# A map's scores of the differential heads in one three-bank PSUM tile, with a softmax over whole rows

## The chip, the cores and the metric

The kernel runs on one core of a Trainium2 chip. Its engines work from queues of their own: TensorE (PE: matrix products, with weight loads shown as PEld), VectorE (DVE), ScalarE (ACT), GpSimd (POOL) and SyncE (SP), which here issues nearly all DMAs. Matrix products land in PSUM, which this kernel uses as eight banks of 512 fp32 columns on 128 partitions. The metric is the device time of one execution in microseconds (us), the median of three runs.

## What is computed

One step of a backbone of two layers over 128 context tokens and 1024 latent tokens, 1024 channels. The first layer is a state-space and pooling mixer, the second one mixes differential attention (8 heads) with windowed attention (16 heads). The change lies in the differential heads. Cut to what matters (the running of `block` over blocks of 128 queries, the projections and the norms are left out):

```python
def diff_attention(q, k, v, lam):
    scale = DIFF_HD ** -0.5

    def block(qb):
        s = jnp.einsum('bhiqd,bhikd->bhiqk', qb, k).astype(jnp.float32) * scale
        p = jax.nn.softmax(s, axis=-1)
        attn = p[:, :, 0] - lam * p[:, :, 1]
        return jnp.einsum('bhqk,bhkv->bhqv', attn.astype(v.dtype), v)
```

A head has two maps (i = 0, 1), each with its own query and key of 64 channels. A latent query reads 128 cached context keys and 1024 latent keys, 1152 in all; the 128 context queries read the 128 context keys.

## The kernel before

Tokens run along the columns of channel-major tiles, in nine blocks of 128 (`NCH`): block 0 is the context, blocks 1 to 8 the latents. Products of fp32 accuracy are made of fp16 pairs (a high and a low part): a projection is three matmuls for each of eight 128-channel slices (`mm3`, lines 330 to 332).

The second layer (`odd`) runs the eight differential heads, then eight blocks of windowed heads, then the output projection. While head h runs its attention, the projections of head h+1 (K, Q and V) and one gate (Z) are worked off by `Filler`: `F.take` hands out projection matmuls to fill TensorE's time between pieces of attention. TensorE's order is the program's; the other engines' orders come from a scheduler, with instructions under `high_priority` put first. `qk_block` projects K or Q and rotates it (`evac`): ScalarE copies the product to `raw`, VectorE multiplies by cosines, VectorE shuffles, GpSimd multiplies by sines and adds, then ScalarE and GpSimd split the result, held in the one buffer `q32`, into its high and low part; SP copies these into the layout that the score matmuls want.

`diff_head` goes over the nine query blocks. For each of the two maps it makes the scores in three chunks of 384 columns (`CH3`; one of 128 for block 0), each chunk in its own PSUM bank (`S1`, which rotates over five banks by `SCORE_BANKS`). VectorE takes a maximum for each chunk (line 1282) and combines the three (1286); ScalarE takes three exponentials with their sums into SBUF (1289). After each map `F.take` gives TensorE a sixteenth of the projections. Then VectorE adds the sums, and combines the two maps in three products (1303); ScalarE and GpSimd split the result into high and low (1306, 1307), and a transposing DMA turns it for the product with the values (1227). That product, `diff_pv`, is put into the queue `pend`, and worked off after the first map of a later block, when more than two entries wait: the block that is three back is done then. It writes into a bank of its own (`sm`), from which ScalarE copies it (1325).

PSUM in this stage: `mm` two banks for projections, `S1` three, `s4` one, `m3` one and `sm` one. The score rotation is these lines:

```python
SCORE_BANKS = ("S1", "s4", "S1", "m3", "S1")
self.banks = {"mm": ["mm"], "S1": list(SCORE_BANKS)}
```

The windowed heads use `mm`, `m3`, `S1`, `s4` and `sm` as well, and take over without a break: the last three value products of head 7 are worked off inside the first windowed block. `odd_setup` loads the cached values (`cv`, lines 1136 to 1141) before the first rotation, through a `q32` buffer.

Of the kernel before, what the change touches and what calls it, by code (L numbers as in the profile page):

```python
# [10 lines left out]
F32 = mybir.dt.float32  # L11
# [37 lines left out]
SCORE_BANKS = ("S1", "s4", "S1", "m3", "S1")  # L49
# [172 lines left out]
class Builder:  # L222
# [291 lines left out]
    def prologue(self):  # L514
# [3 lines left out]
        self.evps.enter_context(self.psum("evps", ss=4, ada=1))  # L518
# [608 lines left out]
    def odd_setup(self):  # L1127
# [8 lines left out]
        self.cv = self.wt([P, 2, 10, P], F16, tag="cv", bufs=1)  # L1136
        t = self.tl(self.rot, [P, TK], F32, "q32", 1)
        nc.sync.dma_start(t, A["cv"])
        cvf = self.cv.rearrange("p a b c -> p a (b c)")
        nc.scalar.activation(cvf[:, 0], t, AF.Copy)  # L1140
        nc.vector.tensor_tensor(cvf[:, 1], t, cvf[:, 0], ALU.subtract)

# [10 lines left out]
        nc.vector.tensor_scalar(self.nsink, self.row("sink"), -1.0, None, ALU.mult)  # L1153

    def qk_block(self, key, src, hs, cache=None, kout=None, scale=1.0, pre=None):
# [7 lines left out]
        def evac(ps, c0, c1):  # L1163
# [7 lines left out]
            nc.vector.scalar_tensor_tensor(q[:, c0 + o:c1], ps[:, o:], scale, self.cosT[:, a:b], ALU.mult, ALU.mult)  # L1171
# [84 lines left out]
    def diff_head(self, h, F):  # L1256
# [8 lines left out]
        for b in range(NCH):  # L1265
            nk = 1 if b == 0 else 9
            w = nk * P
            qs = slice(b * P, (b + 1) * P)
            p = []
            sm = self.wt([P, 16], F32, tag="sms", bufs=6)  # L1270
            part = ((0, P),) if b == 0 else CH3
            for m in range(2):
                ss = []
                mx = self.wt([P, 4], F32, tag="mx", bufs=4)
                nb = sm[:, m:m + 1]
                for j, (c0, c1) in enumerate(part):
                    sv = self.pt("S1")[:, :c1 - c0]
                    o = TC if b else 0
                    for x in range(2):
                        nc.tensor.matmul(sv, q[:, m, x, qs], k[:, m, o + c0:o + c1], start=x == 0, stop=x == 1)  # L1280
                    with self.tc.high_priority():
                        nc.vector.tensor_reduce(out=mx[:, j:j + 1], in_=sv, axis=AX.X, op=ALU.max)  # L1282
                    ss.append(sv)
                pm = self.wt([P, T], F32, tag="p", bufs=4)
                with self.tc.high_priority():
                    nc.vector.tensor_reduce(out=nb, in_=mx[:, 0:len(part)], axis=AX.X, op=ALU.max, negate=True)  # L1286
                    for j, (c0, c1) in enumerate(part):
                        i = 8 + m * 3 + j
                        nc.scalar.activation(pm[:, c0:c1], ss[j], AF.Exp, bias=nb, accum_out=sm[:, i:i + 1])  # L1289
                p.append(pm)  # L1290
                F.take(HEAD_FIRST if b == 0 else left / 16)
                if m == 0:
                    self.pop(2)

            phl = self.wt([P, 2 * T], F16, tag="phl", bufs=2)
            with self.tc.high_priority():
                n = len(part)
                nc.vector.tensor_reduce(out=sm[:, 4:6], in_=sm[:, 8:14].rearrange("p (a b) -> p a b", a=2)[:, :, 0:n],
                                        axis=AX.X, op=ALU.add)
# [7 lines left out]
            nc.gpsimd.tensor_tensor(phl[:, w:2 * w], p[0][:, :w], phl[:, :w], ALU.subtract)  # L1307
# [334 lines left out]
```

## Time and profile before

| | us |
|---|---|
| median of three runs (2294.38 to 2300.79) | 2299.93 |
| the profiled execution | 2299.1 |
| its span, from first to last instruction | 2297.3 |
| TensorE busy (88% of the span) | 2031.8 |
| VectorE busy (67%) | 1534.2 |
| ScalarE busy (56%) | 1293.6 |
| GpSimd busy (46%) | 1067.8 |
| differential heads, first to last score matmul | 679.8 |

The mean granted clock of TensorE is 0.954 of full speed. Busy shares are means over stages with different limits, so what a stage costs is read from its own stretch: how long each engine is busy in it, and in which waits TensorE, which does most of the work, stands still.

### The profile page before, as it was taken

The numbers are of one execution on the slowest core, as the hardware profiler recorded it, in microseconds if no ns is written. First come the engines' busy times: TensorE is split into PE (matmuls) and PEld (weight loads), VectorE is DVE, ScalarE is ACT, GpSimd is POOL, SyncE is SP. The second block draws the span as 40 slices with busy tenths as digits, with TensorE's granted clock in tenths as the row PEclk, the third lists the DMA queues.
The fourth block names the chain that finished last, engine by engine and source line by source line (L and its number), as shares of the span: only waits on it lengthen the run. The fifth ranks groups of instructions, "written<-read, shape, count | busy, mean of one in ns | idle before, by whom it ended". The sixth has DMA issues, their size and how long they took to land. (4 is left out here: it accounts for less than half of the span.)

```text
span 2297.3 us, 50851 instructions
## 1 busy us (share of the span) xinstructions
PE 2031.8 (88%) x20258; PEld 1452.5 (63%) x20258; DVE 1534.2 (67%) x3329; ACT 1293.6 (56%) x3530; POOL 1067.8 (46%) x997
## 2 busy tenths in 40 slices
PE   4997788787999999978898998988977999898997
PEld 2654475564557555656686676775766777686566
DVE  5868989789585444747877777778785545552334
ACT  5575666666363311436666666666676777773321
POOL 1378677876674100134445445345345656552001
PEclk9998899998999999999999999999999999999999
DMA  7221514224657522135555455544556786899412
GB/s 275 70 80 50 147 58 111 82 80 131 222 184 209 174 71 86 40 102 114 97 125 115 96 113 116 105 107 105 105 124 133 151 168 143 171 180 205 155 47 83
DMA packets 434990, 283.17 MB, mean 123 GB/s; under 512 B 374432, under 2 KB 385216, under 8 KB 434752
## 3 DMA queue, kind: packets, MB, share of 16 engines
q1 hardware_dynamic: 433776, 279.34, 49.7%
q8 instruction: 158, 2.59, 0.5%
q10 hardware_dynamic: 976, 0.58, 0.1%
q14 instruction: 80, 0.66, 0.1%
HBM read 133.38 MB, written 29.05 MB: 71 GB/s over the span
## 5 line engine op out<-in xcount | busy, mean ns | idle before, releaser
L330 PE MATMUL psmm<-h,whl 128*128 128x384 f16 (+1 forms) x1104 | 369.9, 336 | 16.7 <-DVE q L1171 11.5
L331 PE MATMUL psmm<-h,whl 128*128 128x384 f16 (+1 forms) x1104 | 368.7, 335 | 2.3 <-DVE h L507 1.7
L332 PE MATMUL psmm<-h,whl 128*128 128x384 f16 (+1 forms) x1104 | 368.7, 335 | 0.0
L330 PE MATMUL psmm<-whl,h 128*128 128x128 f16 x1920 | 345.9, 224 | 0.0
L331 PE MATMUL psmm<-whl,h 128*128 128x128 f16 x1920 | 345.7, 224 | 0.0
L332 PE MATMUL psmm<-whl,h 128*128 128x128 f16 x1920 | 345.4, 224 | 0.0
L330 PEld LDWEIGHTS <-whl 128*128 128x128 f16 x2256 | 226.6, 100 | 162.0 <-issue 23.6
L332 PEld LDWEIGHTS <-whl 128*128 128x128 f16 x2256 | 225.4, 100 | 157.1 <-issue 18.6
L331 PEld LDWEIGHTS <-whl 128*128 128x128 f16 x2256 | 225.9, 100 | 151.6 <-issue 27.6
L1307 POOL TENSOR_TENSOR phl<-p,phl 128x1152 f16<-128x1152 f32 (+1 forms) x72 | 159.9, 2221 | 249.8 <-ACT phl L1306 210.2
L330 PEld LDWEIGHTS <-h 128*128 128x128 f16 x2520 | 250.9, 100 | 9.4 <-issue 3.8
L331 PEld LDWEIGHTS <-h 128*128 128x128 f16 x2520 | 250.8, 100 | 6.9 <-issue 1.2
L332 PEld LDWEIGHTS <-h 128*128 128x128 f16 x2520 | 250.8, 100 | 0.0
L324 DVE SCALAR_TENSOR_TENSOR whl<-w,whl 128x512 f16<-128x512 f32 x248 | 191.0, 790 | 67.6 <-ACT whl L323 67.1
L1385 POOL TENSOR_TENSOR phl<-p,phl 128x1024 f16<-128x1024 f32 (+2 forms) x72 | 135.0, 1876 | 117.6 <-ACT phl L1384 117.2
L323 ACT ACTIVATE whl<-w 128x512 f16<-128x512 f32 x248 | 140.6, 609 | 78.8 <-PE psmm L332 42.3
L1289 ACT ACTIVATE p<-psS,sms 128x384 f32<-128x384 f32 (+1 forms) x240 | 136.0, 569 | 66.0 <-DVE sms L1286 65.6
L1174 POOL TENSOR_TENSOR sw<-sw,sin 128x384 f32<-128x384 f32 (+1 forms) x78 | 87.4, 1121 | 154.2 <-DVE sw L1173 126.4
L1303 DVE SCALAR_TENSOR_TENSOR p<-p,sms,p 128x384 f32<-128x384 f32 (+1 forms) x200 | 151.9, 793 | 2.5
L1282 DVE TENSOR_REDUCE mx<-psS 128x1 f32<-128x384 f32 (+1 forms) x240 | 125.2, 540 | 37.4 <-PE psS L1280 37.4
L1280 PEld LDWEIGHTS <-Q 128*128 128x128 f16 x800 | 73.7, 98 | 117.6 <-issue 82.4
L504 POOL TENSOR_TENSOR h<-mt,h 128x384 f16<-128x384 f32 (+2 forms) x32 | 29.1, 919 | 252.8 <-ACT h L503 252.8
(396 smaller groups left out, 6122.8 us busy)
## 6 DMA issues: line engine op xcount, KB each, us to landing
w<-in_wod SPq DMA_DIRECT2D x52, 512.0 KB, 3.7
w<-in_wev SPq DMA_DIRECT2D x40, 512.0 KB, 4.0
E<-csrow SPq DMA_DIRECT2D x36, 512.0 KB, 3.9
Q<-qhl SPq DMA_DIRECT2D x64, 288.0 KB, 4.6
go_dr<-gl SPq DMA_DIRECT2D x15, 576.0 KB, 3.3
wada<-in_w_ada SPq DMA_DIRECT2D x32, 256.0 KB, 5.4
o<-in_w_ada SPq DMA_DIRECT2D x16, 512.0 KB, 5.8
xT<-in_w_ada SPq DMA_DIRECT2D x16, 512.0 KB, 6.5
```

Of the source, the lines that this page charges most:

```text
L323: nc.scalar.activation(hl[:, 0, a:e], w[:, a:e], AF.Copy if scale is None else AF.Identity, scale=sc)
L324: nc.vector.scalar_tensor_tensor(hl[:, 1, a:e], w[:, a:e], sc, hl[:, 0, a:e], ALU.mult, ALU.subtract)
L330: mm(out, ah, bh, start=start, stop=False)
L331: mm(out, ah, bl, start=False, stop=False)
L332: mm(out, al, bh, start=False, stop=stop)
L1174: nc.gpsimd.tensor_tensor(sw[:, o:], sw[:, o:], self.sinT[:, a:b], ALU.mult)
L1280: nc.tensor.matmul(sv, q[:, m, x, qs], k[:, m, o + c0:o + c1], start=x == 0, stop=x == 1)
L1282: nc.vector.tensor_reduce(out=mx[:, j:j + 1], in_=sv, axis=AX.X, op=ALU.max)
L1289: nc.scalar.activation(pm[:, c0:c1], ss[j], AF.Exp, bias=nb, accum_out=sm[:, i:i + 1])
L1303: nc.vector.scalar_tensor_tensor(p[0][:, c0:c1], p[1][:, c0:c1], sm[:, 2:3], p[0][:, c0:c1], ALU.mult, ALU.add)
L1307: nc.gpsimd.tensor_tensor(phl[:, w:2 * w], p[0][:, :w], phl[:, :w], ALU.subtract)
L1385: nc.gpsimd.tensor_tensor(phl[:, 2 * w:4 * w], p, phl[:, :2 * w], ALU.subtract)
```

## The change

In the differential heads a map's scores go into one PSUM tile of three banks (`S`, 1536 columns, two buffers): 1152 columns of scores as two matmuls of 512 columns and one of 128, for each of the two parts of the query. VectorE takes one maximum over the whole row, ScalarE one exponential with its sum; the first map's exponential goes to SBUF, the second one's is written over its own scores in PSUM. One VectorE product then combines the two, and one ScalarE copy makes the high part. The value product of an earlier block goes into columns 1152 to 1279 of the first map's tile, ahead of that map's scores, and ScalarE copies it out after that map's exponential (`diff_out`). With the two projection banks this is all of PSUM, so the windowed heads' tiles are opened only when the score tiles are closed: the first windowed K and Q and all value products that still wait are finished before that. `m3` moves into the first layer's pool and the windowed heads' one. In the stage ahead of head 0 the projections rotate over `S`, `S`, `mm`, `mm` in place of `m3`, `S1`, `mm`, `mm`. The cached values are loaded after head 0's projections, and head 0's K is rotated from the copy `raw` where its product was made ahead (`pre`). The diff, cut to its core:

```diff
 def pt(self, tag, shape=(P, 512)):
-        p, b = (self.ps, 2 if tag == "mm" else 1) if tag in ("mm", "m3") else (self.ps2, self.psb[tag])
+        p, b = (self.ps, 2) if tag == "mm" else (self.ps2, self.psb[tag])
 def qk_block(self, key, src, hs, cache=None, kout=None, scale=1.0, pre=None):
...
-            nc.vector.scalar_tensor_tensor(q[:, c0 + o:c1], ps[:, o:], scale, self.cosT[:, a:b], ALU.mult, ALU.mult)
+            if pre is None:
+                nc.vector.scalar_tensor_tensor(q[:, c0 + o:c1], ps[:, o:], scale, self.cosT[:, a:b], ALU.mult, ALU.mult)
+            else:
+                nc.vector.tensor_tensor(q[:, c0 + o:c1], raw[:, o:], self.cosT[:, a:b], ALU.mult)
 def diff_head(self, h, F):
...
-            part = ((0, P),) if b == 0 else CH3
             for m in range(2):
-                ss = []
-                mx = self.wt([P, 4], F32, tag="mx", bufs=4)
+                st = self.pt("S", [P, 1536])
+                sv = st[:, :w]
+                out = self.pend.popleft()(st) if m == 0 and len(self.pend) > 2 else None
                 nb = sm[:, m:m + 1]
-                for j, (c0, c1) in enumerate(part):
-                    sv = self.pt("S1")[:, :c1 - c0]
-                    o = TC if b else 0
+                for c0 in range(0, w, 512):
+                    c1 = min(c0 + 512, w)
                     for x in range(2):
-                        nc.tensor.matmul(sv, q[:, m, x, qs], k[:, m, o + c0:o + c1], start=x == 0, stop=x == 1)
-                    with self.tc.high_priority():
-                        nc.vector.tensor_reduce(out=mx[:, j:j + 1], in_=sv, axis=AX.X, op=ALU.max)
-                    ss.append(sv)
-                pm = self.wt([P, T], F32, tag="p", bufs=4)
+                        nc.tensor.matmul(sv[:, c0:c1], q[:, m, x, qs], k[:, m, o + c0:o + c1], start=x == 0, stop=x == 1)
+                e = self.wt([P, T], F32, tag="p", bufs=4)[:, :w] if m == 0 else sv
                 with self.tc.high_priority():
-                    nc.vector.tensor_reduce(out=nb, in_=mx[:, 0:len(part)], axis=AX.X, op=ALU.max, negate=True)
-                    for j, (c0, c1) in enumerate(part):
-                        i = 8 + m * 3 + j
-                        nc.scalar.activation(pm[:, c0:c1], ss[j], AF.Exp, bias=nb, accum_out=sm[:, i:i + 1])
-                p.append(pm)
+                    nc.vector.tensor_reduce(out=nb, in_=sv, axis=AX.X, op=ALU.max, negate=True)
+                    nc.scalar.activation(e, sv, AF.Exp, bias=nb, accum_out=sm[:, 4 + m:5 + m])
+                p.append(e)
+                if out is not None:
+                    out()
                 F.take(HEAD_FIRST if b == 0 else left / 16)
-                if m == 0:
-                    self.pop(2)
...
-                for c0, c1 in part:
-                    nc.vector.scalar_tensor_tensor(p[0][:, c0:c1], p[1][:, c0:c1], sm[:, 2:3], p[0][:, c0:c1],
-                                                   ALU.mult, ALU.add)
-                for c0, c1 in part:
-                    nc.scalar.activation(phl[:, c0:c1], p[0][:, c0:c1], AF.Copy)
+                nc.vector.scalar_tensor_tensor(p[0], p[1], sm[:, 2:3], p[0], ALU.mult, ALU.add)
+                nc.scalar.activation(phl[:, :w], p[0], AF.Copy)
...
+    def diff_pv(self, st, h, b, nk, pt, sm, og, oss):
-        po = self.pt("sm")
+        po = (self.pt("S", [P, 1536]) if st is None else st)[:, T:T + P]
...
+        if st is not None:
+            return lambda: self.diff_out(po, h, b, sm, og, oss)
+        self.diff_out(po, h, b, sm, og, oss)
 def odd(self, hs, pre):
...
-                odps.enter_context(self.psum("odps", S1=3, s4=1, sm=1))
-                self.banks = {"mm": ["m3", "S1", "mm", "mm"]}
+                odps.enter_context(self.psum("dfps", S=2))
+                self.banks = {"mm": ["S", "S", "mm", "mm"]}
                 F.add("first", first(), 28.0)
                 F.until("first")
-                self.banks = {"mm": ["mm"], "S1": list(SCORE_BANKS)}
+                self.banks = {"mm": ["mm"]}
+                self.cached_values()
                 for h in range(8):
...
+                F.until(("wk", 0))
+                F.until(("q", 8))
+                self.pop(0)
+                odps.close()
+                odps.enter_context(self.psum("odps", S1=3, m3=1, s4=1, sm=1))
```

`cached_values` is the load and split of `cv` taken out of `odd_setup`, word for word; `diff_out` is the end of the old `diff_pv` from its copy on.

What this moves, first on VectorE, in a block of a middle head around the first V projection. Before (1282 is the maximum of a chunk, 1286 their combination, 1298 the sum of sums, 1300 and 1301 the scalars of the combination, 1303 the combination itself, 1205 the low part of V):

```order
L1282 TENSOR_REDUCE mx_18091<-pss_2206_18092 128x1
L1298 TENSOR_REDUCE sms_17904<-sms_17904 128x2
L1282 TENSOR_REDUCE mx_18091<-psS_2207_18096 128x1
L1282 TENSOR_REDUCE mx_18091<-psm_2208_18100 128x1
L1300 RECIPROCAL sms_17904<-sms_17904 128x2
L1205 SCALAR_TENSOR_TENSOR V_17950<-psmm_17958,V_17950 128x384
L1286 TENSOR_REDUCE sms_18090<-mx_18091 128x1
L1301 SCALAR_TENSOR_TENSOR sms_17904<-sms_17904,lms_11493 128x1
L1303 SCALAR_TENSOR_TENSOR p_17918<-p_18021,sms_17904,p_17918 128x384 x3
L1282 TENSOR_REDUCE mx_18197<-psS_2215_18198 128x1
```

After (1290 is the maximum of a row, 1299 and 1300 the scalars, 1301 the combination, 1210 the low part of V):

```order
L1301 SCALAR_TENSOR_TENSOR p_17102<-psS_17162,sms_17067,p_17102 128x1152
L1290 TENSOR_REDUCE sms_17230<-psS_17231 128x1
L1210 SCALAR_TENSOR_TENSOR V_17135<-psmm_17143,V_17135 128x384
L1290 TENSOR_REDUCE sms_17230<-psS_17328 128x1
L1210 SCALAR_TENSOR_TENSOR V_17135<-psmm_17279,V_17135 128x384
L1299 RECIPROCAL sms_17230<-sms_17230 128x2
L1300 SCALAR_TENSOR_TENSOR sms_17230<-sms_17230,lms_11488 128x1
L1301 SCALAR_TENSOR_TENSOR p_17265<-psS_17328,sms_17230,p_17265 128x1152
L1290 TENSOR_REDUCE sms_17399<-psS_17400 128x1
```

Before, the maxima of the next block's first map stand ahead of the combination; now each combination stands ahead of them.

Second on SP's queue ahead of head 0 (`q<-in_cv` is the load of the cached values, `q<-in_ckT` that of a head's cached keys, K and Q the copies into the score layout, w a weight block). Before:

```order
L1132 DMA sin_11482<-in_sin 128x1024
L1134 DMA mask_11484<-in_mask 128x896
L1138 DMA q_1358_11487<-in_cv 128x1280
L1161 DMA q_1362_11503<-in_ckT 128x128
L1179 DMA out_dk<-q_1362_11503 128x128
L313 DMA w_1465_12286<-in_wod 128x1024
L1187 DMA K_11717<-qhl_11714 64x1280 x4
```

After:

```order
L1133 DMA mask_11484<-in_mask 128x896
L1163 DMA q_1360_11498<-in_ckT 128x128
L1184 DMA out_dk<-q_1360_11498 128x128
L312 DMA w_1446_12234<-in_wod 128x1024
L1192 DMA K_11712<-qhl_11709 64x1280 x4
L312 DMA w_1468_12595<-in_wod 128x1024
L1197 DMA Q_11825<-qhl_11822 64x2x1152
L312 DMA w_1503_13050<-in_wod 128x1024
L1197 DMA Q_11825<-qhl_11822 64x2x1152 x3
L1152 DMA q_1392_11906<-in_cv 128x1280
L1163 DMA q_1393_11910<-in_ckT 128x128
```

The load has moved from ahead of head 0's keys to behind head 0's queries, and ahead of head 1's keys.

## Rows read from the trace of the kernel before

**Rows 1.** Stretches: us, busy PE PEld DVE ACT POOL, PE clock, DMA, GB/s.

```profile
1038.30:1718.10 679.80, 609.19 (x6807) 476.04 (x6808) 532.32 (x1296) 455.79 (x1390) 310.14 (x185) 0.96 0.52 109
1295.00:1340.00 45.00, 35.33 (x308) 24.86 (x306) 37.92 (x90) 28.44 (x82) 27.78 (x18) 0.95 0.45 98
1340.00:1383.00 43.00, 43.00 (x584) 37.18 (x583) 29.96 (x78) 29.58 (x97) 12.13 (x6) 0.98 0.57 120
1718.10:1741.00 22.90, 19.20 (x183) 13.60 (x182) 14.60 (x42) 14.68 (x50) 11.05 (x9) 1.00 0.53 114
```

**Rows 2.** What line 1280 (scores) waited for: us in total, times.

```profile
  ACT p L1289: 69.1, 36
```

**Rows 3.** TensorE's timeline: start, us, line, operation; idle time before it in brackets.

```profile
1302.49 0.22 PE L1322 MATMUL pssm<-V,PT 128*128 128x128 f16 x1
...
1304.00 0.49 PE L1280 MATMUL pss<-K,Q 128*128 128x384 f16 x2
...
1304.97 0.33 PE L330 MATMUL psmm<-h,whl 128*128 128x384 f16 x1
...
1307.90 0.81 PE L1280 MATMUL psS<-K,Q 128*128 128x384 f16 x4
...
1316.20 0.48 PE L1280 MATMUL psS<-K,Q 128*128 128x384 f16 x2 [2.48 <-ACT p L1289]
...
1322.85 0.48 PE L1280 MATMUL psS<-K,Q 128*128 128x384 f16 x2 [2.59 <-ACT p L1289]
...
1336.09 0.80 PE L1280 MATMUL psm<-K,Q 128*128 128x384 f16 x2 [3.82 <-ACT p L1289]
```

**Rows 4.** Timelines of GpSimd, VectorE and ScalarE just before 1316 us.

```profile
1309.17 2.61 POOL L1182 TENSOR_TENSOR qhl<-q,qhl 128x1280 f16<-128x1280 f32 x1
...
1309.28 2.54 DVE L375 TENSOR_SCALAR rqy<-oss 128x9 int32<-128x9 int32 x1
...
1313.78 1.01 DVE L1282 TENSOR_REDUCE mx<-psS 128x1 f32<-128x384 f32 x2
...
1315.48 0.58 ACT L1289 ACTIVATE p<-psS,sms 128x384 f32<-128x384 f32 x1 [3.38 <-DVE sms L1286]
```

**Rows 5.** Durations: two lines of VectorE (ns min/median/max, whole run), two timeline rows.

```profile
L1303 DVE SCALAR_TENSOR_TENSOR p<-p,sms,p x200: 331/614/2969, 1048.0 to 1723.9; 128x384 f32<-128x384 f32 x96, 128x128 f32<-128x128 f32 x4
L1171 DVE SCALAR_TENSOR_TENSOR q<-psmm,cos x68: 408/547/559, 1003.3 to 2016.0; 128x384 f32<-128x384 f32 x42, 128x256 f32<-128x256 f32 x26
1318.81 1.36 DVE L1243 TENSOR_TENSOR og<-og,orr 128x1152 f32<-128x1152 f32 x1
1735.89 0.67 ACT L1375 ACTIVATE p<-psS,sms 128x512 f32<-128x512 f32 x1
```

**Rows 6.** The stretch behind the 3.82 us wait (columns as in rows 1).

```profile
1338.00:1342.00 4.00, 4.00 (x41) 4.00 (x40) 2.68 (x8) 3.03 (x9) 0.73 (x1) 0.51 0.85 166
```

**Rows 7.** Timelines of SP, ScalarE and TensorE ahead of head 0.

```profile
993.95 0.43 SPq L1138 DMA_DIRECT2D q<-in_cv  x1
...
1000.45 1.27 ACT L1140 ACTIVATE cv<-q 128x1280 f16<-128x1280 f32 x1 [6.36 <-DMA q<-in_cv]
...
1003.89 0.50 PE L330 MATMUL psmm<-h,whl 128*128 128x384 f16 x1 [11.46 <-DVE q L1171]
...
1031.39 2.59 SPq L1192 DMA_DIRECT2D Q<-qhl  x3
...
1038.32 0.37 PE L1280 MATMUL psS<-K,Q 128*128 128x128 f16 x2 [3.64 <-DMA Q<-qhl]
```

**Rows 8.** Timelines of GpSimd and TensorE behind the last differential scores.

```profile
1723.74 2.43 POOL L1307 TENSOR_TENSOR phl<-p,phl 128x1152 f16<-128x1152 f32 x1 [8.35 <-ACT phl L1306]
...
1730.83 0.23 PE L1322 MATMUL pss<-V,PT 128*128 128x128 f16 x1 [1.86 <-DMA PT<-phl]
```

**Rows 9.** VectorE's busy time in lines 1303, then 1282, in 1295 to 1340.

```profile
1295.00:1340.00 45.00, 9.90 (x11) 0.95 0.45 98
1295.00:1340.00 45.00, 11.91 (x24) 0.95 0.45 98
```

More of the change, by code (lines that the diff above doesn't have):

```diff
@@ L48 @@
 WIN_FIRST, WIN_SHIFT = 1.5, 1.0
-SCORE_BANKS = ("S1", "s4", "S1", "m3", "S1")
 NE = 5
@@ L517, in prologue @@
         self.evps = ExitStack()
-        self.evps.enter_context(self.psum("evps", ss=4, ada=1))
+        self.evps.enter_context(self.psum("evps", ss=4, ada=1, m3=1))
         with self.scope("pro"):
@@ L1153, in odd_setup, with cached_values @@
         nc.vector.tensor_scalar(self.nsink, self.row("sink"), -1.0, None, ALU.mult)
+    def cached_values(self):
+        nc, A = self.nc, self.A
+        self.cv = self.wt([P, 2, 10, P], F16, tag="cv", bufs=1)
+        t = self.tl(self.rot, [P, TK], F32, "q32", 1)
+        nc.sync.dma_start(t, A["cv"])
+        cvf = self.cv.rearrange("p a b c -> p a (b c)")
+        nc.scalar.activation(cvf[:, 0], t, AF.Copy)
+        nc.vector.tensor_tensor(cvf[:, 1], t, cvf[:, 0], ALU.subtract)
     def qk_block(self, key, src, hs, cache=None, kout=None, scale=1.0, pre=None):
@@ L1267, in diff_head @@
             w = nk * P
+            o = TC if b else 0
             qs = slice(b * P, (b + 1) * P)
@@ L1291, in diff_head @@
+                if out is not None:
+                    out()
                 F.take(HEAD_FIRST if b == 0 else left / 16)
-                if m == 0:
-                    self.pop(2)
             phl = self.wt([P, 2 * T], F16, tag="phl", bufs=2)
             with self.tc.high_priority():
-                n = len(part)
-                nc.vector.tensor_reduce(out=sm[:, 4:6], in_=sm[:, 8:14].rearrange("p (a b) -> p a b", a=2)[:, :, 0:n],
-                                        axis=AX.X, op=ALU.add)
@@ L1307, in diff_head @@
[L1307 removed]
+                nc.vector.scalar_tensor_tensor(p[0], p[1], sm[:, 2:3], p[0], ALU.mult, ALU.add)
+                nc.scalar.activation(phl[:, :w], p[0], AF.Copy)
+            nc.gpsimd.tensor_tensor(phl[:, w:2 * w], p[0], phl[:, :w], ALU.subtract)
             pt = self.transpose(phl[:, :2 * w], 2 * nk)
[L1309 removed]
@@ L1311, in diff_pv @@
-    def diff_pv(self, h, b, nk, pt, sm, og, oss):
+            self.pend.append(lambda st=None, b=b, nk=nk, pt=pt, sm=sm: self.diff_pv(st, h, b, nk, pt, sm, og, oss))
+    def diff_pv(self, st, h, b, nk, pt, sm, og, oss):
         nc = self.nc
         v = self.R["v", h]
-        po = self.pt("sm")
+        po = (self.pt("S", [P, 1536]) if st is None else st)[:, T:T + P]
         for kb in range(nk):
@@ L1321, in diff_pv, with diff_out @@
                 vh, vl = v[:, 0, 1 + kb], v[:, 1, 1 + kb]
-            nc.tensor.matmul(po[:, :P], pt[:, kb], vh, start=kb == 0, stop=False)
-            nc.tensor.matmul(po[:, :P], pt[:, kb], vl, start=False, stop=False)
-            nc.tensor.matmul(po[:, :P], pt[:, nk + kb], vh, start=False, stop=kb == nk - 1)
-        nc.scalar.activation(og[:, b], po[:, :P], AF.Copy, scale=sm[:, 6:7])
+            nc.tensor.matmul(po, pt[:, kb], vh, start=kb == 0, stop=False)
+            nc.tensor.matmul(po, pt[:, kb], vl, start=False, stop=False)
+            nc.tensor.matmul(po, pt[:, nk + kb], vh, start=False, stop=kb == nk - 1)
+        if st is not None:
+            return lambda: self.diff_out(po, h, b, sm, og, oss)
+        self.diff_out(po, h, b, sm, og, oss)
+    def diff_out(self, po, h, b, sm, og, oss):
+        nc = self.nc
+        nc.scalar.activation(og[:, b], po, AF.Copy, scale=sm[:, 6:7])
         sq = self.wt([P, P], F32, tag="osq", bufs=1)
```

7 lines of the change are left out of this document (removed).

## The prediction

> **What bounds the kernel now.** I first looked at stretches of the span by engine, then at who waited for whom, then at one head instruction by instruction. The differential heads run from 1038.3 to 1718.1 us. In these 679.8 us TensorE is busy for 609.2, so it idles for 70.6, at a mean granted clock of 0.96 of full speed [rows 1]. The waits name the cause: TensorE's score matmuls (L1280) wait 69.1 us, in 36 pieces, for the exponentials (L1289), which release a score bank [rows 2]. Nothing else holds it here. So the stage is TensorE's own work plus this one wait, and the slow clock that follows it.
>
> The wait is periodic. A head has a half in which the next head's K and Q are projected and rotated, and a half for V and the gate. In the first (1295 to 1340 us) TensorE is busy 35.3 of 45.0 us and VectorE 37.9; in the second it is busy all 43.0 us and VectorE 30.0 [rows 1]. All waits of a head lie in the first half: one below 1 us, then 2.48, 2.59 and 3.82 us, and much the same in the other heads [rows 3]. The reason is visible at 1309 to 1316 us: GpSimd holds a 2.61 us operation, a VectorE operation on 9 columns takes 2.54 us beside it, the maxima queue behind that, and the exponentials start only at 1315.48 after 3.38 us of idleness [rows 4]. TensorE then waits for the first of them to give a bank back.
>
> **How much slack there is, before and after.** From rows 3: a whole map's scores take 0.97 us (1304.00 to 1304.97), one share of projection work 2.93 us (1304.97 to 1307.90), the value products of a block 1.51 us (1302.49 to 1304.00). A block is thus 2 x 2.93 + 2 x 0.97 + 1.51 = 9.3 us of TensorE work. Before, five banks serve six chunks, and the third chunk of a map takes the bank of the previous map's first chunk. Between a block's second map and the next block's first, TensorE comes back after 2.93 + 0.65 = 3.6 us. The bank needs three maxima (0.5 each), their combination and one exponential (0.58) [rows 4], some 2.2 us. Slack 1.4 us. A wait of 2.48 us therefore means that the evacuation was late by 3.9, one of 3.82 by 5.2.
>
> After, a map's scores sit in one of two three-bank tiles. The first map's tile A is wanted again by the next block's value products, after 2.93 + 0.97 + 2.93 = 6.8 us; the second map's tile B after 2.93 + 1.51 + 0.97 + 2.93 = 8.3 us. A is held for one maximum over 1152 columns (1.36 us, the 1152-column VectorE row [rows 5]), one exponential (0.67 us for 512 columns against 0.58 for 384 gives some 0.8 ns a column, so 1.2 us [rows 4, 5], and I allow 0.2 for reading its sum) and the copy of the value products (a third of 384 columns, 0.4): 3.2 us, slack 3.6. B is held for maximum, exponential, 0.4 us of scalars and the combination of the two maps (1.36): 4.5 us, slack 3.8. Slack grows from 1.4 to about 3.7 us.
>
> **The change part by part.**
>
> Score waits: lateness of 3.9, 4.0 and 5.2 us against 3.7 of slack leaves 0.2 + 0.3 + 1.5 = 2 us a head, some 15 us over the heads. Without the waits TensorE also arrives sooner, and VectorE has less time to catch up; I take 20 us of waits left, 49 of 69.1 gained. Bounds: 0 left (nothing late beyond 3.7), or 40 left (each removed wait comes back by half at the next map).
>
> VectorE work in this sum: per block six maxima, two combinations of maxima, one of sums and three 384-column products become two maxima and one product. The products now read one operand from PSUM. Today's form, both operands in SBUF, is 0.61 us in the median and up to 2.97; L1171, one operand in PSUM, never takes over 0.56 [rows 5]. I take 1.36 us for the new one, without stretching. The Trainium skill (SBUF — State Buffer, "SBUF: two separate sides") says that a VectorE operation with two SBUF inputs and a GpSimd operation exclude each other for the whole instruction. Rows 5 agree; if the rule did not spare the PSUM form, some 2 us of lateness a head would stay and the 20 us would be 34.
>
> The exponential of the second map is written in place in PSUM. No row shows ScalarE writing there. Nearest is the exponential to SBUF; I take the same 1.2 us. Bounds: 0.6 (faster, hence a small gain) and 2.4 (twice as slow, which takes 1.2 of tile B's 3.8 us slack, perhaps 8 us over the heads). The Trainium skill (ScalarE: Activation LUTs, "Step-by-step: what each stage is for") calls PSUM the quicker destination; by it the sum stands.
>
> Matmuls: columns and instructions are as many as before, 512 + 512 + 128 in place of 3 x 384, so nothing. Value products keep their lag of three entries and move ahead of the first map's scores; TensorE's work is the same, and the transposed weights had been written over two blocks (18 us) earlier, so this costs nothing unless that chain (about 13 us, below) exceeds it.
>
> Clock: 0.96 over 679.8 us is 27 us of full-speed time lost; after the 3.82 us wait the stretch 1338 to 1342 ran at 0.51, that is at 1.2 in place of 2.4 GHz [rows 6]. With two thirds of the waiting gone I take two thirds of it, 18, as gained; bounds 5 and 25.
>
> Start: the cached values' load shares the one buffer of the rotated keys. Issued at 993.95, it held back the first rotation, and TensorE stood 11.46 us until 1003.89 [rows 7]. After, the load follows head 0's queries. TensorE comes, I take, 10.5 us earlier to the key projection of head 1 (11.46 less a us for the tokens it then needs), but there the same buffer is in use by the load: SP issues it behind the Q copies (the last three at 1031.39 for 2.6 us, now 10.5 earlier, so at 1023.5), 6.5 us to land, 1.27 and then about 1.5 us to split [rows 7], 0.95 for two rotating products [rows 5]: the third chunk can start at 1034 with 1.5 us of matmuls ahead of the first scores, at 1035.5 against 1038.32, where they now wait 3.64 us for Q [rows 7]. The wait is moved, not removed: gain 3, bounds -2 and 8.
>
> End: the score tiles are closed before the window heads start, so all value products must be drained, with nothing between. Today TensorE idles only 22.9 - 19.2 = 3.7 us there [rows 1]. After the last scores: maximum 1.36, exponential 1.4, scalars 0.4, product 1.36, split 1.2, GpSimd 2.43, then as from 1726.17 to 1730.83 the transposing copy 4.7 [rows 8]: 12.8 us, under which two blocks' value products (3.0) fit. Idle 9.8 against 3.7, 6 lost, and a slow-clock stretch of some 4 behind it. Loss 10, bounds 5 and 15.
>
> Sum: 49 + 18 + 3 - 10 = 60 us. The profiled execution took 2299.1 us (span 2297.3), 0.8 below the median of the runs, so about 2240 as a median.
>
> **The rivals.**
>
> (1) Lateness carries on: the waits come from queues on VectorE, ScalarE and GpSimd in the rotating half, not from too few banks, and TensorE catches up with the same late engines. For it: the waits occur only in that half [rows 1, 3]. Against: slack grows 2.3 us, about a wait's size. 35 us of waits stay, clock gains 8, start 0, end -12: 34 + 8 - 12 = 30, so 2270.
>
> (2) The wait moves to the two projection banks: Q's first chunk is evacuated only when GpSimd has split K in the one buffer (the 2.61 us operation ends at 1311.78 [rows 4]), and TensorE, no longer held at scores, arrives there sooner. Then 10 of the score waits and 5 of the clock are gained: 10 + 5 + 3 - 10 = 8, so 2291.
>
> (3) Slower: VectorE's chain gets longer than TensorE's block. Its order now has the whole combination of a block ahead of the next block's first maximum: 1.36 + 1.36, an exponential to wait for (1.4), 0.4 and 1.36 make 5.9 us in which it cannot run ahead. Its other work in the rotating half is 37.9 - 9.9 - 11.9 [rows 9], less 3.3 of small reductions, 12.8 us over about four blocks, 3.2 each. If none of it fits into the waiting, a block takes 9.1 us against TensorE's 9.3: it decides from there, with today's 45 / 4 = 11.3 us a block as the point from which it is slower. At 12 us, GpSimd stretching the rest, 32 such blocks lose 22 us, and with the end's 10 less 6 from the start and second halves the time is 2325. For it: VectorE is at 84% in this half. The Trainium skill (PSUM — Partial Sum Buffer, "Engine vs sequencer instructions") says that VectorE's queue is strictly first in, first out; the idle row at 1315.48 agrees, and this rival is what it would do here.
>
> **How the numbers follow.** Forecast 0.61 (2240), rival 1 0.20 (2270), rival 2 0.07 (2291), rival 3 0.12 (2325). About 0.3% (7 us) is what a measurement of this kernel can tell from no change. Faster 0.83, within 0.3% 0.05, slower 0.12. The best bounds together give 69 + 25 + 8 - 5 = 97 us, 2202; the forecast's weak end 29 + 5 - 2 - 15 = 17, 2282. The range 2206 to 2286 leaves out rival 3 and little else.
>
> **What would show it.** Right: waits of L1287 for exponentials or the combination near 20 us, none for projection banks, the rotating half near 38 us at a clock near 1, a TensorE wait of about 10 us before the first scores and one as long at the end. Wrong: waits of tile B for L1301 in every block; exponentials in place over 2 us; products over 1.5 us.

## The result and the profile after

The changed kernel takes 2273.44 us (2269.06 to 2278.25) against 2300.36 (2294.38 to 2302.58) for the kernel before beside it: ratio 0.9887, interval 0.9856 to 0.9919, 27 us less. 2240, 60 us less, had been forecast. The profiled execution took 2269.1 us, its span 2267.3.

Stretches of the changed kernel: the differential heads from first to last scores, the drain behind them, the windowed heads (us, busy PE PEld DVE ACT POOL, clock, DMA, GB/s). The first two answer to [rows 1].

```profile
1030.00:1680.40 650.40, 602.19 (x6807) 459.39 (x6806) 475.16 (x705) 386.15 (x758) 300.70 (x185) 0.97 0.52 114
1680.40:1698.00 17.60, 9.41 (x85) 8.60 (x84) 4.95 (x6) 6.33 (x17) 4.73 (x2) 0.61 0.48 98
1698.00:2052.30 354.30, 322.65 (x4644) 262.91 (x4644) 183.17 (x580) 261.84 (x740) 212.23 (x134) 0.96 0.83 160
```

The differential heads, 679.6 us before (from the start of the first to the start of the last scores, on both sides), take 650.4: 29.2 less where the forecast had 67. TensorE's idle time fell from 70.6 to 48.2 us, its busy time, for the same matmuls, from 609.0 to 602.2; that is the clock. What TensorE waited for in 1030 to 1690, in us, times and longest (1287 scores, 1301 combination, 329 projection matmuls, 1174 rotation, 1210 V's low part); it answers to [rows 2]:

```profile
PE psS L1287 <- DVE p L1301: 31.9, 12, 4.0
PE psmm L329 <- DVE V L1210: 6.8, 6, 2.4
PE psmm L329 <- DVE q L1174: 6.7, 12, 0.6
```

So 31.9 us of waits for tile B and 13.5 for the two projection banks stay; the rest of the 48.2 are waits for tile A. They are again periodic: a middle head (1 to 6 of heads 0 to 7) has 0.63, 0.48 and 2.90 us in the rotating half and up to 2.44 us for V's low part in the other (1.24 in two of the six), and its period is 83.1 us in place of 88.7.

The 2.90 us wait of head 3, read backwards from TensorE's row at 1314.39. The rows are TensorE's, then VectorE's, then ScalarE's (1290 row maximum, 1291 exponential, 379 part of the reciprocal root of a finished head, 1248 and 1249 its two products, 1170 head of a rotated chunk, 1187 GpSimd's split of K):

```profile
1300.54 1.14 PE L1287 MATMUL psS<-K,Q 128*128 128x512 f16 x6
1306.76 1.14 PE L1287 MATMUL psS<-K,Q 128*128 128x512 f16 x6
1314.39 1.21 PE L1287 MATMUL psS<-K,Q 128*128 128x512 f16 x6 [2.90 <-DVE p L1301]
...
1302.81 0.42 DVE L1174 SCALAR_TENSOR_TENSOR q<-psmm,cos 128x256 f32<-128x256 f32 x1 [0.89 <-ACT q L1170]
1303.15 1.68 DVE L379 SCALAR_TENSOR_TENSOR rqy<-rqa,rqy 128x9 f32<-128x9 f32 x1
...
1307.18 1.36 DVE L1248 TENSOR_TENSOR og<-og,orr 128x1152 f32<-128x1152 f32 x1
1308.46 1.35 DVE L1290 TENSOR_REDUCE sms<-psS 128x1 f32<-128x1152 f32 x1
...
1310.67 1.34 DVE L1249 TENSOR_TENSOR og<-og,zs 128x1152 f32<-128x1152 f32 x1
...
1312.92 1.42 DVE L1301 SCALAR_TENSOR_TENSOR p<-psS,sms,p 128x1152 f32<-128x1152 f32 x1
...
1302.50 0.28 ACT L1170 ACTIVATE q<-psmm 128x128 f32<-128x128 f32 x1 [1.01 <-POOL qhl L1187]
...
1309.84 1.20 ACT L1291 ACTIVATE psS<-psS,sms 128x1152 f32<-128x1152 f32 x1 [4.79 <-DVE sms L1290]
```

Tile B's scores end at 1301.7. Their maximum begins at 1308.46, 6.8 us later: it stands on VectorE's queue behind a rotation that waits for ScalarE, which waits for GpSimd, and behind the finished head's chain and first product. The second product then stands ahead of the combination. With nothing in the way the tile would be free after scores, maximum, exponential with its sum, scalars and combination, 1.14 + 1.35 + 1.39 + 0.4 + 1.42 = 5.7 us, at 1306.2. It is free at 1314.3, 8.1 late. TensorE came at 1311.5, so the slack was 5.3, and 8.1 - 5.3 is the wait.

The unit prices came out as taken. Lines of the changed kernel (ns min/median/max):

```profile
L1301 DVE SCALAR_TENSOR_TENSOR p<-psS,sms,p x72: 333/1418/1420, 1035.7 to 1684.1; 128x1152 f32<-128x1152 f32 x64, 128x128 f32<-128x128 f32 x8
L1291 ACT ACTIVATE p<-psS,sms x72: 364/1221/1223, 1030.8 to 1680.7; 128x1152 f32<-128x1152 f32 x64, 128x128 f32<-128x128 f32 x8
L1291 ACT ACTIVATE psS<-psS,sms x72: 323/1195/1197, 1033.7 to 1682.2; 128x1152 f32<-128x1152 f32 x64, 128x128 f32<-128x128 f32 x8
```

### The profile page after: what moved, and what is told of

Read it like the earlier page. It is cut to its first block, busy times and chain, and to the rows that moved or that the text cites. A ratio compares the mean times of both kernels' runs of the same rounds, so it can differ in the third digit from the quotient of the medians.

```text
span 2267.3 us, 49655 instructions
## 1 busy us (share of the span) xinstructions
PE 2025.6 (89%) x20258; PEld 1439.4 (63%) x20258; DVE 1471.5 (65%) x2729; ACT 1223.5 (54%) x2890; POOL 1059.0 (47%) x997
## 5 line engine op out<-in xcount | busy, mean ns | idle before, releaser
L329 PE MATMUL psmm<-whl,h 128*128 128x128 f16 x1920 | 339.7, 222 | 9.7 <-DVE V L1210 6.8
L330 PE MATMUL psmm<-whl,h 128*128 128x128 f16 x1920 | 339.3, 222 | 0.0
L331 PE MATMUL psmm<-whl,h 128*128 128x128 f16 x1920 | 339.1, 222 | 0.0
L323 DVE SCALAR_TENSOR_TENSOR whl<-w,whl 128x512 f16<-128x512 f32 x248 | 196.9, 810 | 63.0 <-ACT whl L322 62.6
L1290 DVE TENSOR_REDUCE sms<-psS 128x1 f32<-128x1152 f32 (+1 forms) x144 | 177.4, 1232 | 51.3 <-PE psS L1287 51.1
L1287 PE MATMUL psS<-K,Q 128*128 128x512 f16 (+1 forms) x800 | 154.7, 328 | 32.0 <-DVE p L1301 31.9
L1302 ACT ACTIVATE phl<-p 128x1152 f16<-128x1152 f32 (+1 forms) x72 | 76.8, 1067 | 105.2 <-issue 39.3
```

The lines of the kernel that those rows point to most:

```text
L323: nc.vector.scalar_tensor_tensor(hl[:, 1, a:e], w[:, a:e], sc, hl[:, 0, a:e], ALU.mult, ALU.subtract)
L329: mm(out, ah, bh, start=start, stop=False)
L330: mm(out, ah, bl, start=False, stop=False)
L331: mm(out, al, bh, start=False, stop=stop)
L1287: nc.tensor.matmul(sv[:, c0:c1], q[:, m, x, qs], k[:, m, o + c0:o + c1], start=x == 0, stop=x == 1)
L1290: nc.vector.tensor_reduce(out=nb, in_=sv, axis=AX.X, op=ALU.max, negate=True)
```

## The experiments

Ratios are to the kernel before, run beside each. "Heads" is the stretch from the first to the last differential scores in the profile, "idle" TensorE's idle time in it, both worked out as above.

| kernel | median us | ratio, interval | heads us | idle us |
|---|---|---|---|---|
| before | 2300.4 | | 679.6 | 70.6 |
| before, norm put off | 2295.6 | 0.9981 (0.9968 to 0.9993) | 677.6 | 69.5 |
| before, norm put off and split later | 2281.1 | 0.9921 (0.9902 to 0.9939) | 664.0 | 62.1 |
| changed | 2273.4 | 0.9887 (0.9856 to 0.9919) | 650.4 | 48.2 |
| changed, norm one place later | 2276.5 | 0.9891 (0.9872 to 0.9911) | 652.7 | 51.7 |
| changed, second exponential to SBUF | 2289.8 | 0.9958 (0.9945 to 0.9970) | 662.3 | 59.4 |
| changed, split later | 2267.6 | 0.9860 (0.9836 to 0.9884) | 648.6 | 47.0 |
| changed, norm put off | 2263.3 | 0.9837 (0.9821 to 0.9854) | 640.0 | 41.8 |
| changed, norm put off and split later | 2237.7 | 0.9731 (0.9716 to 0.9745) | 613.6 | 26.7 |

**Putting off, by the program's order alone.** Theory Q: the chain on VectorE's queue keeps the waits. Norm and gate of a finished head (`diff_norm`) are written into the next head's seventh block, in the changed kernel and in the one before:

```diff
+            if b == 6 and self.late:
+                self.late.popleft()()
...
+        self.late.append(lambda: self.diff_norm(h, og, oss))
...
+    def diff_norm(self, h, og, oss):
```

> The changed kernel, but a finished head's norm and gate (a chain of 9-column VectorE operations, two 1152-column products and the split of the result) are put off from the end of the head, which falls into the next head's rotating half, to the next head's seventh block. Theory Q (the waits that stayed come from VectorE's queue: 4 us of chain and 1.36 us of product stand ahead of a late row maximum): the 2.90 us wait of every head falls below 1 us, the 31.9 us of waits for the combination fall to some 12 (heads 0 and 7 keep theirs), the slow clock behind them goes too; 3 + 1.5 us in 7 heads, some 25 us less, about 2248. Rival H (tile B is held too long, since its exponential is written in place and only the combination frees it): the maximum is early but the hold is as long, a wait of 1.5 us or more stays in each head, at most 10 us less, 2263 or more. Rival M (the work only moves the queue): as much waiting appears in the second half of the head, for the low part of V or for the combination there, 2270 or more.

> The kernel before, with the same putting off of norm and gate to the next head's seventh block, and nothing else changed. Theory Q with room in the changed kernel (the two go together: the queue makes the maxima late, the tiles give slack): of a middle head's four waits (0.78, 2.48, 2.59, 3.82) the 2.48 and the 3.82 behind the chain get shorter, the others stay; 69 us of waits become 40 to 50, time 2270 to 2282. Rival S (with three one-bank chunks the slack of 1.4 us is the limit whatever the queue holds): 60 us or more of waits stay, 2292 or more. Rival Q alone (only the queue matters, the tiles give nothing): 30 us or less stay, 2262 or less, below the changed kernel.

2275.15 us (0.9897, 0.9880 to 0.9915) and 2300.52 (1.0005, 0.9992 to 1.0017). Neither says anything on the theory: in both traces the scheduler had put the chain at its old place on VectorE, with the old waits (2.90 us in the one, 0.77, 2.49, 2.58 and 3.84 in the other). The next pair binds the order.

**Putting off, bound.**

`anchor` is the second row maximum of the block ahead of `diff_norm`; what VectorE does in `diff_norm` is ordered behind it.

```diff
+                with self.tc.issue_after(self.anchor):
+                    self.late.popleft()()
```

> The changed kernel with a head's norm and gate put off again, this time with VectorE's first operation of them ordered behind the second row maximum of the next head's sixth block, since the program's order alone had left VectorE's order as it was (the same chain at the same place, the same 2.90 us wait). Theory Q (the waits that stayed come from the chain and its product ahead of a late row maximum): the 2.90 us wait of every middle head falls below 1 us, the waits for the combination fall from 31.9 to 12 to 16 us (heads 0, 1 and 7 keep theirs), the slow clock behind them goes; some 20 us less, about 2253. Rival M (VectorE's work only moves): waits of 2 us or more a head appear in the half where V and the gate are projected, for V's low part or for the combination; 2268 or more. Rival R (the rotation alone keeps the queue late): a wait of 2 us or more for the combination stays in the rotating half; 2268 or more.

> The kernel before with the same bound putting off and nothing else changed. If queue and banks both count: of a middle head's waits (0.78, 2.48, 2.59, 3.82) those of 2.48 and 3.82 us, behind the chain and its products, fall to half or less, 69 us of waits become 35 to 50, time 2268 to 2285. If the queue alone counts and the tiles give nothing: 30 us or less stay, 2262 or less. If the 1.4 us of slack of the banks is the limit: 60 us or more stay, 2292 or more.

In the changed kernel 10 us, half of what theory Q said; in the one before 3, with 69.5 us of idle time left, the third expectation. In the changed kernel the 2.90 us wait is gone, and two others stand in a middle head. ScalarE's rows ahead of the first, then TensorE's (1186 the split of the rotated Q, 1294 the exponential, 1180 GpSimd's rotation):

```profile
1314.20 1.16 ACT L1186 ACTIVATE qhl<-q 128x1152 f16<-128x1152 f32 x1 [2.74 <-POOL q L1180]
1315.27 1.18 ACT L1294 ACTIVATE psS<-psS,sms 128x1152 f32<-128x1152 f32 x1
...
1319.34 1.15 PE L1290 MATMUL psS<-K,Q 128*128 128x512 f16 x6 [1.33 <-DVE p L1304]
1323.92 0.22 PE L329 MATMUL psmm<-whl,h 128*128 128x128 f16 x1 [2.09 <-DVE V L1210]
```

The maximum was done at 1312.7. The exponential had to wait till 1315.3 behind a split that waited for GpSimd. A second instruction that is late stood at the head of another queue.

**The chain one place later.** The same binding at block 4, so that the chain stands just behind the maximum that it had stood ahead of.

> The changed kernel with norm and gate of the finished head kept in the rotating half, but bound on VectorE to stand just behind the row maximum that it stood ahead of (second map of the next head's fourth block). The same work, one place later. By the trace of the changed kernel this maximum began 6.8 us after its scores had ended, and the combination freed tile B 8.1 us later than with nothing in the way, against 5.2 us of slack: 2.9 us of wait. Theory O (the order decides: one maximum takes all the lateness): the 2.90 us wait falls below 1 us and no new one over 1.5 us appears in a middle head, 5 to 12 us less, 2261 to 2268. Rival W (the amount of work in that half decides): a wait of 2 us or more for tile B or A appears one or two maps later, within 5 us of 2273.

2276.46 us: rival W. The maximum for tile B is on time, and a middle head now has a wait of 4.79 us, for tile A:

```profile
1314.99 3.52 DVE L1248 TENSOR_TENSOR og<-og,orr 128x1152 f32<-128x1152 f32 x1
1318.43 1.34 DVE L1293 TENSOR_REDUCE sms<-psS 128x1 f32<-128x1152 f32 x1
...
1322.60 0.35 ACT L1331 ACTIVATE og<-psS,sms 128x128 f32<-128x128 f32 x1
...
1323.00 0.26 PE L1322 MATMUL psS<-V,PT 128*128 128x128 f16 x1 [4.79 <-ACT og L1331]
```

Moving the chain within the rotating half gave nothing; the lateness fell on the next map. Some of the 4.79 us is a new price: the chain's first product took 3.52 us here, 1.36 in the changed kernel. By these numbers about 2.6 us (an estimate, 4.79 less 2.16) would have been left without that.

**Tile B freed by the exponential.** The second exponential writes its own SBUF tile, so the hold ends with it.

```diff
-                e = self.wt([P, T], F32, tag="p", bufs=4)[:, :w] if m == 0 else sv
+                e = self.wt([P, T], F32, tag="p", bufs=4)[:, :w]
```

> The changed kernel, but the second map's exponential goes to its own SBUF tile, so that tile B is free after the exponential and the combination reads both maps from SBUF. Theory Q: in the 2.90 us wait the exponential of the late map ended at 1311.0 and TensorE arrived at 1311.5, so this wait goes, but the late maximum stays and so do the queues, and the combination is stretched beside GpSimd (a mean above 1.7 us in place of 1.42); 10 to 18 us less, 2255 to 2263. Rival H (the hold alone is the limit): all waits for tile B go, in head 7 too, 30 us less or more, 2243 or less. Rival L (the read from PSUM is what keeps the combination short, and the stretched one makes VectorE the bound): waits come back for other reasons, 2273 or more.

2289.81 us, 16 more than the changed kernel: the third expectation. The maximum is as late as before. The 2.90 us wait is gone, and one of 4.20 us for tile A has come. TensorE, not held at tile B, comes to tile A that much sooner, and the combination, now reading both maps from SBUF, is stretched to 2.24 us there, beside a GpSimd operation that is stretched too; the next map's maximum and exponential stand behind it:

```profile
L1301 DVE SCALAR_TENSOR_TENSOR p<-p,sms,p x72: 332/1419/3430, 1039.6 to 1701.9; 128x1152 f32<-128x1152 f32 x64, 128x128 f32<-128x128 f32 x8
...
1313.46 1.35 DVE L1290 TENSOR_REDUCE sms<-psS 128x1 f32<-128x1152 f32 x1
...
1317.93 2.24 DVE L1301 SCALAR_TENSOR_TENSOR p<-p,sms,p 128x1152 f32<-128x1152 f32 x1
...
1318.91 3.48 POOL L510 TENSOR_TENSOR gl<-og,gl 128x1152 f16<-128x1152 f32 x1
...
1324.51 0.26 PE L1319 MATMUL psS<-V,PT 128*128 128x128 f16 x1 [4.20 <-ACT og L1328]
```

The hold alone is not the limit. The combination took 1.42 us at most with an operand in PSUM and up to 3.43 without; 19 of the 64 wide ones were stretched, by 16 us in all. That agrees with the Trainium skill (SBUF — State Buffer, "SBUF: two separate sides"), by which a VectorE operation with two SBUF inputs and a GpSimd operation that reads SBUF shut each other out for a whole instruction. That the stretching is the whole of the 16 us lost is not shown: of the 4.20 us wait it is 0.8.

**The split behind the next exponential.** On top of the bound putting off, `qk_block` hands the end of a Q block (split, copies, `R[key]`) to the next map:

```diff
+        if self.lazy and cache is None:
+            self.tails.append(tail)
...
+                if self.tails:
+                    with self.tc.issue_after(last_e):
+                        self.tails.pop()()
```

> The kernel with the bound putting off, and ScalarE's split of the rotated queries put behind the next exponential on ScalarE. In that kernel's trace the exponential of a late map stood behind this split, which waited 2.74 us for GpSimd's rotation; TensorE waited 1.32 us for the combination behind it and 2.09 us for V's low part. Theory C (each wait that is left comes from one instruction at the head of an in-order queue): the 1.32 us wait goes in the six middle heads, the 2.09 us wait shrinks; with little clock to gain 8 to 14 us less than that kernel's 2263, 2249 to 2255. Rival M (waits move on): the 1.32 goes but waits of the same sum appear elsewhere in the half, 2260 or more.

2237.65 us, 25.7 less than with the putting off alone, where theory C said 8 to 14. A middle head now takes 78.2 us at full clock and has two waits of note, 0.6 us for a projection bank and 1.30 for tile A:

```profile
1246.00:1324.20 78.20, 76.07 (x895) 58.70 (x895) 59.11 (x93) 49.59 (x98) 38.73 (x25) 1.00 0.56 123
...
1324.23 0.22 PE L1334 MATMUL psS<-V,PT 128*128 128x128 f16 x1 [1.30 <-ACT og L1343]
```

Of the 26.4 us that the heads lost against the putting off alone, 15.0 are idle time and 11.4 TensorE's busy time, the clock. The wait for V's low part fell from 2.09 to 0.3 with it.

**Do the tiles count at all, and does one late order hide the other?**

> The kernel before with both repairs of the order together: norm and gate bound to the next head's seventh block, ScalarE's split of the rotated queries behind the next exponential (here behind the three exponentials of a map). In the changed kernel the two took the differential heads from 650.4 to 613.6 us. If the queues are all there is and the tiles give nothing: the waits fall from 69 to 25 us or less, the heads to some 630, time 2252 or less. If the 1.4 us of slack of three one-bank chunks is a limit of its own: 45 us or more of waits stay and the time is 2275 or more. In between the tiles' worth is what is left against 2237.6.

> The changed kernel with the later split of the queries alone, norm and gate left where they were. If each late order costs on its own and their gains add: the putting off gave 10.1 us and the two together 35.8, so the split alone would give some 20 to 26 (2247 to 2253). If the first late instruction hides the second (the 2.90 us wait for the norm's chain comes before the split's place and takes the time that the split would have cost): 8 us or less, 2265 or more.

The kernel before with both repairs: 2281.1 us, 62 us of waits left in the heads, the second expectation. The biggest of a middle head is 4.85 us (1250 the second product, 510 the split of the result, 1301 an exponential, 1292 scores):

```profile
1340.44 2.82 DVE L1250 TENSOR_TENSOR og<-og,zs 128x1152 f32<-128x1152 f32 x1
...
1343.30 1.16 ACT L510 ACTIVATE gl<-og 128x1152 f16<-128x1152 f32 x1 [3.05 <-DVE og L1250]
1344.37 0.56 ACT L1301 ACTIVATE p<-psS,sms 128x384 f32<-128x384 f32 x1
...
1345.07 0.48 PE L1292 MATMUL psS<-K,Q 128*128 128x384 f16 x2 [4.85 <-ACT p L1301]
```

The same work put off to the same block costs a middle head of the changed kernel the 1.30 us above. So the change is worth 29.2 us of the heads as the order stood (679.6 - 650.4) and 50.4 with both repairs (664.0 - 613.6). How much of that is the slack of the two tiles, and how much the shorter work on rows (VectorE is busy for 475 us of the heads in place of 532, ScalarE for 386 in place of 456), no run here separates. The split alone gives 6 us, the putting off alone 10, both 36: the chain's wait hides the split's, and the other way round, as the second expectation for the split alone had it.

**The start.** The cached values come in halves through two tiles of the score pool:

```diff
-        t = self.tl(self.rot, [P, TK], F32, "q32", 1)
...
+        for a, b in ((0, 640), (640, TK)):
+            t = self.wt([P, T], F32, tag="p", bufs=4)[:, :b - a]
```

> The changed kernel, but the cached values are loaded through two tiles of the score pool in place of the one buffer of the rotated keys, from the same place in the program. The prediction's step at the start (the wait of 11.5 us is moved, not removed): the 11.70 us wait ahead of head 0's first scores falls to the 3.6 us wait for Q that the kernel before had, or below; 7 to 9 us less, about 2265. Rival (the wait is not the load's: TensorE would wait there for the rotation or for Q as long): less than 3 us, 2270 or more.

2264.59 us (0.9848, 0.9833 to 0.9862), 8.8 less: the wait was the load's. What is left is the wait for Q that the kernel before had [rows 7]:

```profile
1021.01 0.29 PE L1288 MATMUL psS<-K,Q 128*128 128x128 f16 x2 [2.90 <-DMA Q<-qhl]
```

**The end.** A gate projection moved from the windowed heads to head 7, 6 us of it kept for the drain (`add_z(8 + qb)` for `add_z(7 + qb)`, `F.take` between the last pops).

> The changed kernel with one gate projection (head 7's) moved from the windowed heads to head 7, and 6 us of projection work kept back and handed out between the value products that are drained before the windowed tiles open. The prediction's step at the end (the drain has nothing under it): the three waits of 1.71, 2.38 and 3.64 us there fall to under 2 us in all, and head 7's four waits for the combination (2.01, 3.29, 1.97, 1.87) shrink by half, since a block has more projection work; 10 us less before the windowed heads, of which these, with 11.8 us less to fill with, give back 3 to 8 us: 2264 to 2271. Rival (the drain is bound by its own chain, not by missing work, or the windowed heads give all of it back): 2273 or more.

2304.83 us, 31 more than the changed kernel: the rival, by far. The drain and the windowed heads:

```profile
1683.60:1701.30 17.70, 8.69 (x120) 8.09 (x119) 4.84 (x7) 6.80 (x18) 3.68 (x2) 0.71 0.44 96
1701.30:2085.10 383.80, 325.27 (x4459) 262.12 (x4459) 188.12 (x579) 262.67 (x739) 220.62 (x134) 0.94 0.71 147
```

The drain took 17.7 us in place of 17.6 though it had projection work, its last wait for the transposing copy 6.38 in place of 3.64 us: it is bound by its own chain. The windowed heads, with less to fill, took 383.8 us in place of 354.3; TensorE's idle time there went from 31.6 to 58.5. In head 7, which had the projection, the waits for the combination fell as expected, from 9.1 us in four to 3.2 in one.

**Together.** Putting off, cached values and the moved projection, then the first two, then these two with the later split:

> The changed kernel with the bound putting off, the cached values loaded through two tiles of the score pool, and the gate projection moved to the end of the differential heads, together. If the three costs are apart from one another their gains add: 8.8 us for the load as measured, 20 for the queue if theory Q holds, 2 to 9 for the end: some 2238. If the queue's part falls (rivals M or R): 2258 to 2265.

> The bound putting off and the cached values through two tiles of the score pool, without the moved gate projection. The moved projection alone cost 31 us against the changed kernel, and the three together were at 2285. If the parts add, this one is at 2254 (2273.4 less 8.8 less 10.1, or 2285 less 31). Rival (the two gains are one and the same time): 2260 or more.

> The bound putting off, the later split and the cached values through the score pool together. If theory C holds and the parts add: 2240 to 2246. If the later split gives nothing: 2254.

2285.0, 2250.85 and 2227.46 us. The parts add, the moved projection as a loss of 34, for which the first missed its 2238. The last was 13 us under its range, since the later split gave more than had been expected. It (ratio 0.9682, 0.9668 to 0.9697) beats the kernel before by 71 us and the changed one by 46.

## Why the prediction was right in sign and wrong in size

**Score waits: here it failed.** The step that failed is "lateness of 3.9, 4.0 and 5.2 us against 3.7 of slack leaves" 2 us a head, from which 20 us of waits were to be left. The slack was not the fault: it was 5.3 us at the place above, more than the 3.7 taken, 1.1 of it TensorE's own waits for projection banks. The lateness was. It was read from the trace of before and taken as a property of the stage, when it is one of the order in the queues, and the change made a new order: one row maximum for a map in place of three, and the whole chain, a product and a rotation ahead of it. Before, some 13 us of lateness a head were spread over three maps; now 8.1 fall on one. And the waits for the projection banks, which the forecast put at none, are 13.5 us. In all TensorE idles 48.2 us in the heads, not 20: 22.4 us gained where 49 had been forecast. That the chain made the map late is shown by the bound putting off, in which the 2.90 us wait is gone; that its place alone does not decide, by the chain one place later, which took 2276.5 us. With the two late orders repaired the heads take 613.6 us; the forecast was 679.8 - 67 = 612.8. That is no rescue of the step: 15.6 us of it the repairs give to the kernel before as well.

**Clock: 18 forecast, 6.8 seen** (busy 609.0 to 602.2). It was taken in proportion to the waits, and so most of this miss is the step above again: the 22.4 of 70.6 us of idle time that went would by the same proportion have given 8.6 of 27. A middle head's one 2.90 us wait still brings the lower of the two levels (1.2 in place of 2.4 GHz) behind it, as 3.82 us did [rows 6]:

```profile
1314.40:1318.40 4.00, 4.00 (x35) 3.53 (x36) 2.24 (x3) 3.90 (x7) 4.00 (x2) 0.62 0.34 133
```

In the kernel with both repairs, whose middle heads wait 1.30 us at most, busy time is 586.9, 22 less than before.

**Prices: right.** Maximum 1.35, exponential 1.22 to SBUF and 1.195 in place, combination 1.418 and never stretched; no bound was needed.

**Start: right.** From the issue of the cosines' load (979.52 and 974.32) to the first scores (1038.32 and 1029.98) it took 58.8 us and now 55.7, 3.1 less for 3 forecast. The wait of 11.5 us came back as 11.70 behind the load, at the place named:

```profile
1016.65 1.58 SPq L1152 DMA_DIRECT2D q<-in_cv  x1
...
1023.64 1.27 ACT L1154 ACTIVATE cv<-q 128x1280 f16<-128x1280 f32 x1 [7.61 <-DMA q<-in_cv]
...
1027.15 0.48 PE L329 MATMUL psmm<-h,whl 128*128 128x384 f16 x1 [11.70 <-DVE q L1174]
```

**End: right in kind, 6 lost for 10.** The scores of the windowed heads:

```profile
L1362 PE MATMUL psS<-K,Q x288: 216/326/421, 1718.1 to 2084.1; 128*128 128x384 f16 x96, 128*128 128x256 f16 x32, 128*128 128x128 f16 x16
L1365 PE MATMUL psS<-K,Q x288: 216/326/326, 1698.0 to 2052.4; 128*128 128x384 f16 x96, 128*128 128x256 f16 x32, 128*128 128x128 f16 x16
```

From the last differential to the last windowed scores it took 366.2 us (1717.9 to 2084.1) and now 372.0 (1680.4 to 2052.4), 5.8 lost. The drain idles nearly as forecast, for 8.2 us, of which 1.71, 2.38 and 3.64 us are its waits for tile A and for the transposing copies, with the clock at 0.61 over it. The windowed heads give some back, being 11.6 us shorter: 3.9 since the value products of the last blocks lie in the drain, the rest TensorE's idle time. Over the whole stretch TensorE idles 0.5 us more than before and is busy 5.3 us longer, so what was lost is the slow clock.

The terms are 29.2 + 3.1 - 5.8 = 26.5, beside the 27 of the medians. The profiled executions differ by 30, as the part ahead of the change is 5.2 us shorter in this one; in the traces of the changed kernel and its variants the issue of the cosines' load lies between 971.1 and 980.1.

**The rivals.** The first, lateness carries on (2270, 35 us of score waits), is what happened: 2273, 31.9 us for tile B. The second, the projection banks, came as 13.5 us beside it: 6.7 for the rotation, by the mechanism named, and 6.8 for V's low part, which it did not name. The third named the right engine: VectorE's order is what made a map 8.1 us late. It did not make the kernel slower: waits for the combination in block after block came in head 7 alone (2.01, 3.29, 1.97 and 1.87 us), which has a projection less to fill with and lost three of the four when it was given one. The range was said to leave out the third rival "and little else"; it leaves out the second's 2291 too, and its ends lie 4 us above the 2202 and 2282 worked out.

## What to carry to other kernels

A wait behind an in-order queue has two sizes, the slack of the buffer, which can be counted from the code, and the lateness of the instruction that frees it, which belongs to the order and must be read anew from the changed kernel's order, with all that stands ahead of it. Where several late instructions stand on the way, removing one only shows the next, so a gain is counted when all are found. Where a scheduler decides the order, writing code later may move nothing; bind the instruction.

## What was not expected of the hardware

The clock's loss goes with TensorE's idle time only down to a point. Against the 586.9 us of busy time with both repairs, the kernel before lost 22.1 us at 70.6 us of idle time and the changed one 15.3 at 48.2, which is the same share. But the middle heads of the changed kernel, each taken from one 2.90 us wait to the next, had a granted 0.96 to 0.98 at 4.1 to 6.5 us of idle time, and those with both repairs, whose waits are 1.30 us at most, 1.00 at 2.1 us (the row of 1246 to 1324.2). Head 2 of the changed kernel:

```profile
1231.00:1314.00 83.00, 78.93 (x895) 60.70 (x895) 60.98 (x93) 49.67 (x98) 38.96 (x25) 0.96 0.52 116
```

And where a product of two SBUF operands stands in the queue changes its price: the first product of the gate took 1.36 us where GpSimd was idle and 3.52 beside its 2.37 us split at 1314.92, the second 2.82, beside another such split at 1339.68, in place of 1.34.
